# A decoder trunk on one core: the first products put between the transposes of the two halves of the input, and fewer small operations in 1/rms and the final norm

## The chip, the core and the metric

The kernel runs on one core of a Trainium2 chip. The metric is device time in microseconds (us) of one execution, given as the median of three runs. Five engines work beside each other, each through a queue of its own in a fixed order: TensorE (PE; its weight loads are shown as PEld), VectorE (DVE), ScalarE (ACT), GpSimd (POOL), and SyncE (SP), which here only issues transfers. Queues meet at semaphores: an instruction that waits holds up everything behind it on its engine.

## What is computed

The reference is a decoder trunk of two layers on 512 positions with 1024 features. Each layer is a gated linear attention (layer 0) or a stick-breaking attention (layer 1) between two half-step SwiGLU feed-forward blocks; a norm ends it.

```python
def rmsnorm(x, g):
    y = x * lax.rsqrt(jnp.mean(x * x, axis=-1, keepdims=True) + EPS)
    return y * g

def swiglu(h, w_gate, w_up, w_down):
    return (jax.nn.silu(h @ w_gate) * (h @ w_up)) @ w_down

def reference(x, ...):
    for i in range(2):
        x = x + 0.5 * swiglu(rmsnorm(x, ffn1_norm[i]), ffn1_w_gate[i], ffn1_w_up[i], ffn1_w_down[i])
        h = rmsnorm(x, mix_norm[i])
        x = x + (gla_mixer(h, ...) if i == 0 else sb_mixer(h, ...))
        x = x + 0.5 * swiglu(rmsnorm(x, ffn2_norm[i]), ffn2_w_gate[i], ffn2_w_up[i], ffn2_w_down[i])
    return rmsnorm(x, final_norm)
```

The feed-forward width is 2816. Inputs and output are float32.

## The kernel before

**Layout.** The running x is kept transposed in eight tiles `xs[k]` of 128 features by 512 positions. Every product runs on pairs: a value is split into a rounded part (`h`, made by a cast on ACT) and the rest (`l`, value minus `h`, made on DVE), and `mm3` issues three matmuls, `wh*h`, `wl*h` and `wh*l`. One column of 128 outputs over 1024 features is thus 8 x 3 = 24 matmuls of 512 positions, made by `feat`. Its accumulators rotate over eight PSUM banks.

**Feed.** All weight products stand in one list, `feed.q`. Each entry has weights to be split (`split`: `wh` cast on ACT, `wl` subtraction on DVE, four buffers of each) and a generator `body` that issues its matmuls in two halves. Taking an entry with `start` also splits the two that follow and loads further ones.

**The norm.** The products begin before the norm's 1/rms is known: the input is multiplied by the gain alone, the sums of squares run aside, and the factor comes in later. `two_halves(stats_a)` issues the first two columns (48 matmuls) and between their halves `stats_a`, which calls `rstd` for the 1/rms of 512 positions as a 128 x 4 tile (`rv`, square root `ry` on ACT, reciprocal, `rq`, `r4`). `stats_b` makes four diagonal tiles `dg` and multiplies them by ones on PE, which gives `ps_R`, a bank with the factor in every row; `R` is its copy. Then the first two columns, kept back in their banks, are multiplied by `R` (`flush`), and DVE and ACT make the normed tiles `xn`, `nh`, `nl` and their sums and differences `ts`, while PE works on the third to sixth columns. The seventh column is the first that reads `nh` and `nl`. From the third chunk of weights on a scheme with seven products in place of eight is used (`seven`).

**The start.** x arrives as eight blocks (four of positions, two halves of features; SP's queue, with the first weight between the halves). One transpose of the 50 rows of gains gives `gT`. Then, for all eight `k`, four transposes fill a bank, ACT writes `xh` (bank times gain), DVE writes `xl`, and a copy (ACT and DVE by turns) keeps the bank in `xs[k]`. The squares of the blocks run on ACT with their sums in `sums`. The program states the order of few of these; a scheduler places the others, and an `issue_after` in the source puts an instruction behind another one.

**The end.** The last block's down product is made by positions. For each of four position tiles `last` runs twice, for the left (`dh` 0) and the right half: add to x, square with a sum, and after the second half `rstd` of one column, scaling of both halves, and two transfers to the output.

Of the kernel before, what the change touches and what calls it, by code (L numbers as in the profile page):

```python
# [18 lines left out]
P = 128  # L19
T = 512  # L20
# [12 lines left out]
def decoder(ctx: ExitStack, tc: tile.TileContext, a: dict, out: bass.AP):  # L33
# [29 lines left out]
    def mm(ps, l, r, first, last):  # L63
        nc.tensor.matmul(ps, l, r, start=first, stop=last)  # L64
# [27 lines left out]
    class Entry:  # L92
# [8 lines left out]
        def split(self):  # L101
            if self.W is None:
                self.W = []
                for ch, view, n, m in self.units:
# [14 lines left out]
                    st["cut"] = nc.scalar.copy(h, r).ins  # L119
                    with tc.issue_after(st["gains"]):  # L120
                        nc.vector.tensor_tensor(out=l, in0=r, in1=h.bitcast(F32), op=ALU.subtract)  # L121
# [52 lines left out]
    def feat(ch, f, evac, tag=None, defer=None):  # L174


        def body(W):
            (wh, wl), = W
            ps = psum("ps_f", tag)
            for part in (range(0, KD // 2), range(KD // 2, KD)):  # L180
                for k in part:
                    mm3(ps, wh[:, k], wl[:, k], st["h"][k], st["l"][k], k == 0, k == KD - 1)
                if part[-1] == KD - 1:
# [183 lines left out]
    def rstd(sums, n):  # L367
        v = sp.tile([P, n], F32, tag="rv", bufs=2, name="rv")
        nc.vector.tensor_scalar(out=v, in0=sums, scalar1=1.0 / D, scalar2=EPS, op0=ALU.mult, op1=ALU.add)
# [4 lines left out]
        nc.vector.tensor_tensor(out=q, in0=y, in1=y, op=ALU.mult)  # L374
        nc.vector.tensor_tensor(out=q, in0=q, in1=v, op=ALU.mult)
        nc.vector.tensor_scalar(out=q, in0=q, scalar1=-0.5, scalar2=1.5, op0=ALU.mult, op1=ALU.add)
# [17 lines left out]
    def two_halves(between=None):  # L394

        feed.finish()
        g = [feed.start(), feed.start()]
# [24 lines left out]
    class FFN:  # L422
# [10 lines left out]
        def __init__(self, wg, wu, wd, gi, nxt, first=False, last=False):  # L433
# [6 lines left out]
            for group, (c0, c1) in enumerate(self.GROUPS):  # L440
                slots, put = 2 * (c1 - c0), 0
                for i in range(slots):
# [14 lines left out]
                    elif c not in self.SEVEN_UP:  # L457
                        feat(g, f_, self.evac_g, defer=d)
# [194 lines left out]
        def run(self, between=None):  # L653
            with tc.tile_pool(name="hp", bufs=8, reuse_waits="tile") as self.hp, tc.tile_pool(
# [4 lines left out]
                two_halves(stats_a)  # L659
# [509 lines left out]
    def to_tokens(tp):  # L1169
        fin = st["fin"] = tp.tile([P, D], F32, tag="s", bufs=4, name="fin")  # L1170
# [13 lines left out]
    def last(dh, i, ps):  # L1184
# [7 lines left out]
        if dh == 0:  # L1192
            nc.vector.tensor_tensor(out=x, in0=x, in1=fin[:, 0:T], op=ALU.mult)
            return
        s = st["sq"][:, 2 * i : 2 * i + 1]
        nc.vector.tensor_tensor(out=s, in0=s, in1=sq, op=ALU.add)
        r = rstd(s, 1)
        nc.vector.scalar_tensor_tensor(out=x, in0=x, scalar=r, in1=fin[:, T:D], op0=ALU.mult, op1=ALU.mult)
        nc.sync.dma_start(rows[:, T:D], x)
        nc.scalar.activation(xt[i, 0], xt[i, 0], AF.Copy, scale=r)  # L1200
        nc.sync.dma_start(rows[:, 0:T], xt[i, 0])
# [12 lines left out]
    with tc.tile_pool(name="ip", bufs=1) as ip:  # L1214
        gl = ip.tile([P, P], F32, name="gl")
        nc.vector.memset(gl, 0.0)
        row = 0
        for nm in ("ffn1_norm", "mix_norm", "ffn2_norm"):
# [39 lines left out]
        for e in feed.q[:2]:  # L1258
            e.split()
# [53 lines left out]
```

## Time and profile before

| | us |
|---|---|
| runs | 1871.04, 1872.98, 1873.69 |
| median | 1872.98 |
| the profiled execution's own time | 1871.49 |
| its span, first to last instruction | 1869.6 |

In the profile's rows a time is from the span's start. A timeline row has start, duration, engine, source line, operation, output and input tiles with their shape, how many equal ones follow each other (x), and in brackets how long the engine sat idle before it and what ended that. An engine name with q is its queue issuing a transfer. Durations overlap: the next instruction can start before the last one has drained, so prices are taken from start to start. A group's row has a count, busy time and mean.

### The profile page before, as it was taken

To read this page: it belongs to the slowest core of one execution; us is meant where nothing else is said; L and a number is where in the kernel's file an instruction comes from. 1 tells how busy PE (TensorE), PEld (TensorE's weight loads), DVE (VectorE), ACT (ScalarE), POOL (GpSimd) and SP (SyncE) were. 2 spreads that over 40 slices of the span, in tenths; PEclk is the share of its full clock that TensorE was granted. 3 is DMA by queue.
4 is the path that set the end of the run, shared out by engine and by line. 5 is a ranking of instruction groups with operands and counts; after the bars stand their busy time and mean duration, and the time that the engine had idled before them with its cause. 6 is when DMAs were issued, how large, how long until landed. Compare 5 with 4: busy or idle time off the path is not lost.

```text
span 1869.6 us, 28889 instructions
## 1 busy us (share of the span) xinstructions
PE 1849.7 (99%) x11789; PEld 1647.6 (88%) x11789; DVE 1456.8 (78%) x2313; ACT 954.0 (51%) x1506; POOL 7.3 (0%) x17
## 2 busy tenths in 40 slices
PE   8999999999999999999999999999999999999998
PEld 6899999789887899999888999998888788999997
DVE  7978777775766988877888778776878769778785
ACT  6534434444555544444554444445888755444444
POOL 0000000100000000000000000000000000000000
PEclk9999999999999999999999999999999999999999
DMA  5423333212223233342233333233221223333321
GB/s 158 146 91 112 103 113 105 86 50 65 64 72 113 77 104 103 108 129 80 79 113 124 102 102 113 79 93 100 68 68 57 68 91 95 120 102 102 119 85 68
DMA packets 177514, 179.03 MB, mean 96 GB/s; under 512 B 4035, under 2 KB 167925, under 8 KB 177381
## 3 DMA queue, kind: packets, MB, share of 16 engines
q1 hardware_dynamic: 176768, 176.18, 30.1%
q8 instruction: 92, 1.51, 0.3%
q0 software_dynamic: 512, 0.99, 0.2%
q14 instruction: 42, 0.34, 0.1%
q10 hardware_dynamic: 100, 0.03, 0.0%
HBM read 175.11 MB, written 2.10 MB: 95 GB/s over the span
## 4 chain that ended last, share of the span: by engine, by line
PE 96%; DVE 2%; ACT 1%; DMA 1%; issue 0%; DVEq 0%; ACTq 0%; SPq 0%
PE ps_d L64 25%; PE ps_f L64 20%; PE ps_w L510 15%; PE ps_z L510 10%; PE ps_q L510 10%; PE ps_t L64 5%; PE ps_b L64 4%; PE ps_S L64 1%; PE ps_z L1044 1%; PE ps_bt L64 1%; PE ps_oT L1106 1%; PE ps_T L1091 1%; PE ps_o L64 1%; DVE wl L121 0%; DMA raw<-in_ffn_w_up_dram 0%; PE ps_R L64 0%
## 5 line engine op out<-in xcount | busy, mean ns | idle before, releaser
L121 DVE TENSOR_TENSOR wl<-raw,wh 128x1024 fp32r<-128x1024 f32 x244 | 261.3, 1071 | 81.8 <-ACT wh L119 71.6
L119 ACT CAST wh<-raw 128x1024 fp32r<-128x1024 f32 x244 | 226.5, 932 | 137.4 <-PE ps_f L64 44.3
L64 PE MATMUL ps_d<-hh,wl 128*128 128x512 f32 x672 | 262.1, 390 | 0.0
L64 PE MATMUL ps_d<-hh,wh 128*128 128x512 f32 x672 | 262.1, 390 | 0.0
L64 PE MATMUL ps_d<-hl,wh 128*128 128x512 f32 x672 | 261.4, 389 | 0.0
L119 ACT CAST wh<-s 128x1024 fp32r<-128x1024 f32 x136 | 142.8, 1050 | 142.4 <-PE ps_q L510 70.4
L297 DVE SCALAR_TENSOR_TENSOR x<-ps_d,x 128x512 f32<-128x512 f32 x184 | 125.6, 688 | 87.6 <-PE ps_d L64 87.4
L121 DVE TENSOR_TENSOR wl<-s,wh 128x1024 fp32r<-128x1024 f32 x136 | 166.2, 1222 | 25.9 <-ACT wh L119 15.3
L64 PE MATMUL ps_f<-xh,wh 128*128 128x512 f32 x448 | 181.7, 406 | 3.1 <-DVE q L707 1.5
L64 PE MATMUL ps_f<-xl,wh 128*128 128x512 f32 x448 | 175.0, 391 | 0.0
L64 PE MATMUL ps_f<-xh,wl 128*128 128x512 f32 x448 | 174.5, 389 | 0.0
L119 ACT CAST wh<-rawd 128x1024 fp32r<-128x1024 f32 x84 | 88.5, 1054 | 150.7 <-PE ps_d L64 127.6
L510 PE MATMUL ps_z<-th,wh 128*128 128x256 f32 x544 | 150.3, 276 | 0.0
L510 PE MATMUL ps_z<-th,wl 128*128 128x256 f32 x544 | 150.2, 276 | 0.0
L510 PE MATMUL ps_z<-tl,wh 128*128 128x256 f32 x544 | 150.1, 276 | 0.0
L510 PE MATMUL ps_w<-nh,wl 128*128 128x256 f32 x544 | 150.1, 276 | 0.0
L510 PE MATMUL ps_w<-nl,wh 128*128 128x256 f32 x544 | 150.1, 276 | 0.0
L64 PEld LDWEIGHTS ps_d<-hl,wh 128*128 128x128 f32 x672 | 126.2, 188 | 26.7
L64 PEld LDWEIGHTS ps_d<-hh,wh 128*128 128x128 f32 x672 | 126.2, 188 | 24.8
L64 PEld LDWEIGHTS ps_d<-hh,wl 128*128 128x128 f32 x672 | 126.1, 188 | 24.1
L121 DVE TENSOR_TENSOR wl<-rawd,wh 128x1024 fp32r<-128x1024 f32 x84 | 102.9, 1225 | 42.8 <-ACT wh L119 33.6
L510 PE MATMUL ps_w<-nh,wh 128*128 128x256 f32 x488 | 134.7, 276 | 0.0
(249 smaller groups left out, 4711.7 us busy)
## 6 DMA issues: line engine op xcount, KB each, us to landing
raw<-in_ffn_w_gate_dram SPq DMA_DIRECT2D x43, 1024.0 KB, 5.4
raw<-in_ffn_w_up_dram SPq DMA_DIRECT2D x43, 1024.0 KB, 5.3
rawd<-in_ffn_w_down_dram SPq DMA_DIRECT2D x84, 512.0 KB, 3.5
raw<-in_gla_w_in_dram SPq DMA_DIRECT2D x12, 1024.0 KB, 5.3
raw<-in_sb_w_in_dram SPq DMA_DIRECT2D x16, 512.0 KB, 3.8
raw<-in_gla_w_out_dram SPq DMA_DIRECT2D x4, 1024.0 KB, 5.1
raw<-in_sb_w_in_dram SPq DMA_DIRECT2D x4, 1024.0 KB, 5.1
raw<-in_sb_w_out_dram SPq DMA_DIRECT2D x4, 1024.0 KB, 5.0
```

The lines of the kernel that those rows point to most:

```text
L64: nc.tensor.matmul(ps, l, r, start=first, stop=last)
L119: st["cut"] = nc.scalar.copy(h, r).ins
L121: nc.vector.tensor_tensor(out=l, in0=r, in1=h.bitcast(F32), op=ALU.subtract)
L297: nc.vector.scalar_tensor_tensor(out=xs[k], in0=ps, scalar=0.5, in1=xs[k], op0=ALU.mult, op1=ALU.add)
L510: nc.tensor.matmul(o, l_, r_, start=first and j + n == 0, stop=j == 3 and n == 2, skip_group_check=True)
L1044: nc.tensor.matmul(o_, l_, r_, start=first, stop=last, skip_group_check=True)
L1091: nc.tensor.transpose(ps[:, c0 : c0 + P], ys[yb][:, yc + j * P : yc + (j + 1) * P], ident)
L1106: nc.tensor.matmul(po[e * 64 : e * 64 + 64, j * P : T], self.v[j][:, c : c + 64], self.wt[p, e][bk][:, c0 : c0 + n], start=j == 0, stop=j ...
```

## The change

The start is written in an explicit order. The gains come in two tiles, `gls[0]` with the 16 rows that the first block needs and `gls[1]` with the rest. `turn(0)` transposes the left half of the features, then the first gain tile, and writes `xh`, `xl` of `k` 0 to 3. The first weight is split behind the third of these evacuations (`behind` is an `issue_after` on several instructions), the kept copies come behind that split, and the first column's body runs its first part, now three of eight `k` (nine matmuls). Behind the last of them on PE stands `turn(1)` with the right half's sixteen transposes; then the second weight's split, its copies, the splits that `feed.start()` makes, six of the eight squares, the rest of the first column and the second gain transpose. Since the first column is done, `two_halves` takes one column for the first block. In the built kernel ACT's queue runs, from the start: two squares, four `xh`, the first weight's cast, two copies, four `xh`, the second weight's cast, two copies, the third's cast, six squares, the fourth's cast, a table load, the square root and the casts of the fifth, sixth and seventh columns. On DVE the splits of the fifth and sixth columns stand between the reciprocal and the end of 1/rms. On PE `ps_R` stands behind 18 matmuls of the third column. SP's queue keeps its order up to the output. Behind the first 80 us or so the queues are as before until the last norm.

`rstd` keeps the sum of squares undivided (the constants take the factor), can add a second sum in its first operation, and for one column multiplies twice in one operation. `last` writes the left half times the final gain to a tile of its own, `xf`, and sends it from ACT's queue.

```diff
     def mm(ps, l, r, first, last):
-        nc.tensor.matmul(ps, l, r, start=first, stop=last)
+        st["pe"] = nc.tensor.matmul(ps, l, r, start=first, stop=last).ins
...
-                    st["cut"] = nc.scalar.copy(h, r).ins
-                    with tc.issue_after(st["gains"]):
-                        nc.vector.tensor_tensor(out=l, in0=r, in1=h.bitcast(F32), op=ALU.subtract)
+                    st["cut"] = (
+                        nc.scalar.copy(h, r).ins,
+                        nc.vector.tensor_tensor(out=l, in0=r, in1=h.bitcast(F32), op=ALU.subtract).ins,
+                    )
...
-            for part in (range(0, KD // 2), range(KD // 2, KD)):
+            for ks in (range(0, part), range(part, KD)):
...
-    def rstd(sums, n):
+    def rstd(sums, n, more=None):
         v = sp.tile([P, n], F32, tag="rv", bufs=2, name="rv")
-        nc.vector.tensor_scalar(out=v, in0=sums, scalar1=1.0 / D, scalar2=EPS, op0=ALU.mult, op1=ALU.add)
+        nc.vector.tensor_scalar(
+            out=v, in0=sums, scalar1=0.0 if more is None else more, scalar2=D * EPS, op0=ALU.add, op1=ALU.add
+        )
...
-        nc.vector.tensor_tensor(out=q, in0=y, in1=y, op=ALU.mult)
-        nc.vector.tensor_tensor(out=q, in0=q, in1=v, op=ALU.mult)
-        nc.vector.tensor_scalar(out=q, in0=q, scalar1=-0.5, scalar2=1.5, op0=ALU.mult, op1=ALU.add)
+        if n == 1:
+            nc.vector.scalar_tensor_tensor(out=q, in0=y, scalar=v, in1=y, op0=ALU.mult, op1=ALU.mult)
+        else:
+            nc.vector.tensor_tensor(out=q, in0=y, in1=y, op=ALU.mult)
+            nc.vector.tensor_tensor(out=q, in0=q, in1=v, op=ALU.mult)
+        c = float(D) ** 0.5
+        nc.vector.tensor_scalar(out=q, in0=q, scalar1=-0.5 * c, scalar2=1.5 * c, op0=ALU.mult, op1=ALU.add)
...
-                        feat(g, f_, self.evac_g, defer=d)
+                        feat(g, f_, self.evac_g, defer=d, part=3 if len(feed.q) == 0 else KD // 2)
...
-                two_halves(stats_a)
+                two_halves(stats_a, 2 - (feed.pos == 1))
...
         if dh == 0:
-            nc.vector.tensor_tensor(out=x, in0=x, in1=fin[:, 0:T], op=ALU.mult)
+            st["xf"] = st["tp"].tile([P, T], F32, tag="s", bufs=4, name="xf")
+            nc.vector.tensor_tensor(out=st["xf"], in0=x, in1=fin[:, 0:T], op=ALU.mult)
             return
-        s = st["sq"][:, 2 * i : 2 * i + 1]
-        nc.vector.tensor_tensor(out=s, in0=s, in1=sq, op=ALU.add)
-        r = rstd(s, 1)
+        r = rstd(sq, 1, st["sq"][:, 2 * i : 2 * i + 1])
         nc.vector.scalar_tensor_tensor(out=x, in0=x, scalar=r, in1=fin[:, T:D], op0=ALU.mult, op1=ALU.mult)
         nc.sync.dma_start(rows[:, T:D], x)
-        nc.scalar.activation(xt[i, 0], xt[i, 0], AF.Copy, scale=r)
-        nc.sync.dma_start(rows[:, 0:T], xt[i, 0])
+        nc.scalar.activation(st["xf"], st["xf"], AF.Copy, scale=r)
+        nc.scalar.dma_start(rows[:, 0:T], st["xf"])
...
+        def turn(hf):
+            pst = []
+            for k in range(hf * 4, hf * 4 + 4):
+                ps = psum("ps_x")
...
+                pst.append(ps)
+            if hf == 0:
+                ps = psum("ps_g")
+                nc.tensor.transpose(ps[:, 0:P], gls[0], ident)
+                nc.vector.tensor_copy(gT[:, 0:16], ps[:, 0:16])
+            for k, ps in enumerate(pst, hf * 4):
...
+                turned.append(c)
+            return pst
...
+        squares(0, (0, 1))
+        pst = turn(0)
+        with behind(turned[2]):
+            feed.q[0].split()
+        with behind(st["cut"]):
+            keep(pst, 0)
+        body = feed.q[0].body(feed.q[0].W)
+        next(body)
+        with tc.issue_after(st["pe"]):
+            pst = turn(1)
+        with behind(turned[5]):
+            feed.q[1].split()
+        with behind(turned[7]):
+            keep(pst, 1)
+            feed.start()
+        with behind(st["cut"]):
+            squares(0, (2, 3))
+            squares(1, range(NT))
+        for _ in body:
+            pass
+        ps = psum("ps_g")
+        with tc.issue_after(st["pe"]):
+            nc.tensor.transpose(ps[:, 0:P], gls[1], ident)
+        nc.vector.tensor_copy(gT[:, 16:50], ps[:, 16:50])
```

69 lines of the change are left out of this document (37 added, 32 removed).

## The prediction

> **What bounds the kernel now.** I read the page first: TensorE (PE) is busy for nearly the whole span, so only the stretches in which it is idle or slow can pay or cost.
>
> ```profile
> PE 1849.7 (99%) x11789; PEld 1647.6 (88%) x11789; DVE 1456.8 (78%) x2313; ACT 954.0 (51%) x1506; POOL 7.3 (0%) x17
> ```
>
> Of the 1869.6 us span, 20 us are left, and the waits of PE put 6.0 of them before its first instruction. The change touches the first 50 us and the last 8, so I read the timeline of both, PE first.
>
> ```profile
> 6.00 0.45 PE L1234 MATMUL ps_g<-ident,gl 128*128 128x128 f32 x1 [6.00 <-DMA gl<-in_ffn_norm_dram]
> 6.24 3.41 PE L1241 MATMUL ps_x<-ident,x 128*128 128x128 f32 x15
> ```
>
> ```profile
> 12.19 3.00 PE L1241 MATMUL ps_x<-ident,x 128*128 128x128 f32 x13 [0.25 <-DMA x<-in_x_dram]
> 14.87 0.54 PE L64 MATMUL ps_f<-xh,wh 128*128 128x512 f32 x1
> 15.25 0.40 PE L64 MATMUL ps_f<-xh,wl 128*128 128x512 f32 x1
> 15.49 0.40 PE L64 MATMUL ps_f<-xl,wh 128*128 128x512 f32 x1
> ```
>
> ```profile
> 1836.34 3.65 PE L1177 MATMUL ps_T<-ident,x 128*128 128x128 f32 x32
> ```
>
> The reader is to see two speeds. At the end 32 transposes start (3.65-0.27)/31 = 0.109 us apart (0.27: one transpose there); at the start (3.41-0.42)/14 = 0.214 apart. So PE runs at half rate at the start, and it does so until the last transpose; the first products (14.87, 15.25, 15.49) already come at 0.38 and 0.24. Whatever lifts PE to full rate, before has paid it with transposes; the products are spared.
>
> **The change part by part.** The two ends come from different work: the tail is a serial chain, the start is a reordering. The sum is made against the profiled execution's 1871.49 us, which lies 1.49 under the median of 1872.98.
>
> *Tail.* The last tile's chain on VectorE (DVE) loses the addition of the two sums and one of the two multiplications.
>
> ```profile
> 1863.36 0.16 DVE L1196 TENSOR_TENSOR gT<-gT 128x1 f32<-128x1 f32 x1 [0.85 <-ACT ps_bt L1190]
> 1863.55 0.15 DVE L369 TENSOR_SCALAR rv<-gT 128x1 f32<-128x1 f32 x1
> ```
>
> ```profile
> 1864.17 0.16 DVE L374 TENSOR_TENSOR rq<-ry 128x1 f32<-128x1 f32 x1
> 1864.37 0.16 DVE L375 TENSOR_TENSOR rq<-rq,rv 128x1 f32<-128x1 f32 x1
> ```
>
> ```profile
> 1865.69 0.33 SPq L1201 DMA_DIRECT2D out_dram<-x  x1
> 1866.12 0.38 SPq L1199 DMA_DIRECT2D out_dram<-x  x1
> ```
>
> ```profile
> q1 hardware_dynamic: 288, 0.52, 41.0%
> ```
>
> Nothing covers this chain, so each removed step is worth its start-to-start: 0.19 + 0.20 = 0.39 us. The second output transfer goes to ScalarE's (ACT's) queue, so it is issued up to 1866.12-1865.69 = 0.43 earlier. The DMA line covers 1865.5 to 1868.9: 41% of 3.4 us is 1.4 us of all 16 engines for these two transfers, and they ran one behind the other, so a joint issue shares the same engines. I take 0 for it (bounds 0 and -0.43). The issue takes a place in ACT's queue, where only the next tile's first square stands behind it, and nothing behind the last tile's: hidden. Copying into a new tile xf costs nothing: same operation, and its fourth buffer waits for an output sent three tiles earlier. Tail: -0.4 us (bounds -0.2, -0.8). For the four-column 1/rms the number of operations is unchanged, so the other norms give 0.
>
> *Start, step 1: up to the first product.* PE no longer waits for all four gain loads, but the first 16 transposes need the fourth block of x.
>
> ```profile
> 6.34 0.63 ACT L1264 ACTIVATE junk<-x 128x512 f32<-128x512 f32 x1
> 6.49 0.21 DVE L1235 COPY gT<-ps_g 128x50 f32<-128x50 f32 x1 [5.45 <-PE ps_g L1234]
> ```
>
> ```profile
> 9.05 1.05 ACT L119 CAST wh<-raw 128x1024 fp32r<-128x1024 f32 x1 [1.98 <-DMA raw<-in_ffn_w_gate_dram]
> ```
>
> ```profile
> 16.21 1.32 ACT L1246 ACTIVATE xh<-ps_x,gT 128x512 fp32r<-128x512 f32 x2
> 17.36 0.64 ACT L1257 COPY x<-ps_x 128x512 f32<-128x512 f32 x1
> 17.82 1.12 ACT L119 CAST wh<-raw 128x1024 fp32r<-128x1024 f32 x1
> 18.77 0.70 ACT L1264 ACTIVATE junk<-x 128x512 f32<-128x512 f32 x1
> 19.30 0.26 ACT L1264 ACTIVATION_READ_ACCUMULATOR junk<-x 128x1 f32 x1
> 19.39 0.65 ACT L1257 COPY x<-ps_x 128x512 f32<-128x512 f32 x1
> ```
>
> ```profile
> 16.10 2.72 DVE L1247 SCALAR_TENSOR_TENSOR xl<-ps_x,gT,xh 128x512 fp32r<-128x512 f32 x4
> 18.73 1.28 DVE L1255 COPY x<-ps_x 128x512 f32<-128x512 f32 x2
> 19.93 1.22 DVE L121 TENSOR_TENSOR wl<-raw,wh 128x1024 fp32r<-128x1024 f32 x1
> ```
>
> These rows give the start-to-start prices: on ACT an xh (17.36-16.21)/2 = 0.575, a kept copy 0.46, a cast 0.95, a square 0.62; on DVE an xl 0.66, a copy 0.60. The block is read at 6.34 by ACT, so it has landed by then: fourth transpose at 6.3, twelve more at 0.214 end at 8.9, and only then stands the gain transpose, at 9.1. Its copy follows 0.49 later and takes 0.21, so the first xh starts at 9.9 (before: 11.48). But the new order puts all four xh ahead of the first weight's cast: 9.9+4x0.575 = 12.2, although that weight was there at 9.05. The cast ends at 13.25 and frees the first product; wl ends 1.22 later, at 14.5, and the second product waits for it. So the products gain 0.8 us at most (15.25 to 14.5), and behind nine of them stand sixteen transposes that before had behind it by then.
>
> *Step 2: at what rate PE runs there.* After the gain transpose PE is idle from 9.5 to 13.3. I take it to be at half rate at 14.5 again and to need as much unbroken work as before had directly ahead of its first full-rate product: 14.87-12.19 = 2.7 us, so until 17.2. Six products at an estimated 0.44 (0.228 times 0.214/0.109), two at 0.228, sixteen transposes at 0.109: 17.6, then 19.35. Bounds: no slow work after 14.5 (18.1), or slow for 8.9 us as from 6.00 to 14.87 (21.3).
> The Trainium skill ("TensorE: Matmul & The Clock Gate", Part 1) has the rule for this: an idle PE gets half its clock, and gets all of it after a busy window of about 3.4 us that runs free of the kernel. The factor of two agrees with the trace, while the page's clock row (tenths, all 9) does not show the slow spell.
>
> *Step 3: the first two columns.* The second half's xh run at 18.4 and every 0.575, xl behind them at 0.66, and PE uses them in that order: it is the later, 19.35+15x0.228 = 22.8. The second weight is cast at 20.7, its wl is done at 23.0; so no wait, and 0.24 for the second gain transpose plus 24x0.228 put 48 products at 28.5. In before they end where the R product starts, 26.69: 1.8 late.
>
> *Step 4: R.* In the built order of the changed kernel ACT runs after the last xh (to 20.7): cast, two copies, cast, six squares, cast, table load, square root. DVE has two further weight splits (wl, of columns four and five) between the reciprocal and the rest of 1/rms. In before one split stands ahead of the reciprocal and none behind it.
>
> ```profile
> 23.50 1.28 ACT L371 ACT_TABLE_LOAD   x1
> ```
>
> ```profile
> 23.98 1.22 DVE L121 TENSOR_TENSOR wl<-raw,wh 128x1024 fp32r<-128x1024 f32 x1
> 25.11 0.17 DVE L372 RECIPROCAL ry<-ry 128x4 f32<-128x4 f32 x1
> ```
>
> ```profile
> 25.91 0.16 DVE L378 TENSOR_TENSOR r<-ry,rq 128x4 f32<-128x4 f32 x1
> 26.18 0.87 DVE L387 TENSOR_SCALAR dg<-ident,r 128x128 f32<-128x128 f32 x4
> ```
>
> ```profile
> 26.69 1.06 PE L64 MATMUL ps_R<-dg,gT 128*128 128x128 f32 x8
> 27.50 0.47 PE L64 MATMUL ps_f<-xh,wh 128*128 128x512 f32 x1
> 27.78 0.69 DVE L392 COPY R<-ps_R 128x512 f32<-128x512 f32 x1 [0.72 <-PE ps_R L64]
> ```
>
> ACT: 20.7+0.95+0.93+0.95+6x0.62 = 27.25, cast 28.2, table 1.28, root at 29.5, reciprocal at 29.8. The first split waits for its cast, which stands behind the root (29.75+1.05 = 30.8), and takes 1.13; 0.2 for a small operation, the second split 1.13, then 0.4 to r, 0.27 to dg, 0.51 to PE: R at 34.45. PE has done the 18 products that stand ahead of R at 28.5+18x0.228 = 32.6. It waits 1.85 us; queued behind R are the six last products of the third column, and every product after. Next product: 34.45+0.81 = 35.3; in before the same product came at 27.50+18x0.228 = 31.6. Now 3.7 late.
>
> *Step 5: the normed input.* R now comes with 78 products left before the normed tiles are used, in before with 96.
>
> ```profile
> 49.39 0.39 PE L64 MATMUL ps_f<-nh,wh 128*128 128x512 f32 x1
> ```
>
> ```profile
> 48.99 0.76 DVE L608 TENSOR_TENSOR ts<-xn 128x256 f32<-128x256 f32 x2
> 49.70 1.29 DVE L599 TENSOR_TENSOR nl<-xn,nh 128x512 fp32r<-128x512 f32 x2
> ```
>
> DVE works without a break from R's copy (27.78) to the fourth nl (50.39): 22.6 us. PE wants that nl eleven products after 49.39, at 51.9: 1.5 to spare. After: the queue has one split (1.13) and two differences (0.67) less, so 20.8 from 35.55, that is 56.4; PE wants it at 35.3+89x0.228 = 55.6. Another 0.8 us (bounds 0 and 1.5). Behind it DVE is no later than PE by more than that, so nothing further.
>
> Sum: 3.7+0.8-0.4 = +4.1 us: 1875.6 for a profiled execution, 1877.1 as a median. By the bounds of step 2 alone it is +2.7 to +5.6.
>
> **The rivals.**
> *Full rate at once.* The first product already lifts the rate, as 14.87 to 15.25 (0.38, then 0.24) would allow: one product there was enough. Decides if the products from 14.5 on come 0.23 apart. Then transposes end at 18.1, 48 products at 27.2, R (bound by ACT and DVE) at 33.05: +3.1-0.4 = +2.7, 1875.7. That is not slower by a measurement's 0.2% (3.7 us, about what can be told from no change here). For it: the records show full rate from the second product. Against: half rate for 8.9 us just before it.
> *A long slow spell.* PE idles for 3.8 us between 9.5 and 13.3, which never happens in before, and starts afresh: slow to 20.6 or beyond, all nine products and the transposes; 48 products at 30.1 to 30.9, while R moves with them: +5.3 to +5.6, about 1878.4. For it: 8.9 us of half rate from 6.00. Against: that work had waits in it.
> By the skill's window the full clock would come between 17.9 and 21.3 here, an estimate from that page's 3.4 us, which is +4.4 to +5.5 in all.
> *The splits are no obstacle.* If R needed neither split (an idle DVE queue), step 4's wait and step 5's go and +1.5 stays, 1874.5. Against it stands the written order of the queue; nothing for it but error in my durations.
> *Faster by 0.2%.* It would take 3.7 us out of what precedes the second product; the twelve transposes behind the fourth block at full rate would bring the xh forward by 12x0.105 = 1.3, no more. I find no mechanism for it.
>
> **How the numbers follow.** Forecast 0.5, full rate at once 0.22, long slow spell 0.18, no obstacle 0.06, faster 0.04. The forecast lies just above 0.2%, so 0.33 of its 0.5 counts as slower; with 0.18 that makes 0.51; same is 0.17+0.22+0.06 = 0.45; faster 0.04. The range takes in the rivals from 1875.7 to 1878.6 and the spread of the median about them (1.3 us either way): 1874.4 to 1879.9.
>
> **What would show it.** Right: the first product at about 13.3 and the second at 14.5; products 0.4 apart there; a wait of PE for DVE dg of 1 to 2 us at about 33; a short wait for nl at about 56; last DVE chain two operations shorter. Wrong: products at 0.23 from 14.5 on (step 2), no wait at R (step 4), an R product before 32, or an end of 48 products before 27.

## The result, and the profile after

The change makes the kernel slower: 1879.12 us median of seven runs (1877.72 to 1880.09) against 1872.32 us of the kernel before on the same chip, a ratio of 1.0035 with a 95% interval of 1.0023 to 1.0047. That is 6.8 us, where 4.1 were forecast. The profiled execution took 1879.43 us with a span of 1877.7, 8.1 us over the span before. One of the eleven runs of the last experiment below took 1896.99 us at a granted clock of 0.948, and its ratio and interval include that run.

TensorE's line of the page and its timeline at the start, of the changed kernel:

```profile
PE 1853.0 (99%) x11790; PEld 1648.7 (88%) x11790; DVE 1456.3 (78%) x2307; ACT 952.3 (51%) x1506; POOL 7.3 (0%) x17
```

```profile
13.58 0.80 PE L64 MATMUL ps_f<-xh,wh 128*128 128x512 f32 x1 [3.65 <-ACT wh L120]
14.84 0.79 PE L64 MATMUL ps_f<-xh,wl 128*128 128x512 f32 x1 [0.47 <-DVE wl L121]
...
17.56 0.63 PE L64 MATMUL ps_f<-xh,wl 128*128 128x512 f32 x1
17.99 0.47 PE L64 MATMUL ps_f<-xl,wh 128*128 128x512 f32 x1
18.30 1.91 PE L1267 MATMUL ps_x<-ident,x 128*128 128x128 f32 x16
```

PE is no busier in share, but by 3.3 us (1853.0 against 1849.7) with one matmul more: some work ran slowly. The products behind 14.84 come up to 17.99 0.43 us apart (the first of them 0.59), those behind them 0.23, and the sixteen transposes behind them take 1.67 us (18.30 to the next product at 19.97): full rate from about 18.2. The norm's factor, PE and then DVE:

```profile
34.67 1.16 PE L64 MATMUL ps_R<-dg,gT 128*128 128x128 f32 x8 [1.33 <-DVE dg L395]
35.58 0.47 PE L64 MATMUL ps_f<-xh,wh 128*128 128x512 f32 x1
```

```profile
30.38 0.18 DVE L376 RECIPROCAL ry<-ry 128x4 f32<-128x4 f32 x1 [0.29 <-ACT ry L375]
31.31 1.23 DVE L121 TENSOR_TENSOR wl<-raw,wh 128x1024 fp32r<-128x1024 f32 x1 [0.76 <-ACT wh L120]
...
32.53 1.22 DVE L121 TENSOR_TENSOR wl<-raw,wh 128x1024 fp32r<-128x1024 f32 x1
...
34.33 0.87 DVE L395 TENSOR_SCALAR dg<-ident,r 128x128 f32<-128x128 f32 x4
```

The two splits stand where the forecast put them, between the reciprocal and the rest of 1/rms. The product behind R starts at 35.58; the same one started at 31.71 before, so PE is 3.9 us late. At the normed input two short waits follow:

```profile
54.51 0.50 PE L64 MATMUL ps_f<-nh,wl 128*128 128x512 f32 x1 [0.51 <-DVE wl L121]
...
57.37 0.51 PE L64 MATMUL ps_f<-nl,wh 128*128 128x512 f32 x1 [0.21 <-DVE nl L607]
```

Set against the same products of before, PE is 4.0 us late at 50 us and 5.4 at 60. It stays there, within 0.2 us, for 540 us. Then comes a place that the forecast did not look at: the first products of layer 0's second feed-forward block. PE's timeline there, of before and then of after, and windows of after (length, busy time of PE, PEld, DVE, ACT and POOL with counts, the granted clock, the share of the DMA engines, GB/s):

```profile
599.39 0.50 PE L64 MATMUL ps_f<-xh,wh 128*128 128x512 f32 x1 [1.20 <-DVE x L232]
...
605.19 0.97 PE L64 MATMUL ps_st<-gT,ss 128*128 128x1 f32 x8
```

```profile
610.74 1.05 PE L64 MATMUL ps_st<-gT,ss 128*128 128x1 f32 x8 [1.31 <-DVE ss L342]
...
612.72 0.63 PE L64 MATMUL ps_f<-xh,wh 128*128 128x512 f32 x1
613.14 0.63 PE L64 MATMUL ps_f<-xh,wl 128*128 128x512 f32 x1
```

```profile
608.67:612.08 3.41, 2.10 (x14) 1.59 (x13) 1.48 (x4) 1.97 (x3) 0.00 (x0) 1.00 1.07 348
612.08:615.49 3.41, 3.41 (x10) 2.63 (x9) 2.85 (x10) 1.19 (x2) 0.00 (x0) 0.50 0.15 48
```

The reader is to see a wait that changed its place. Before, PE waits 1.20 us in front of the second column. In the changed kernel the scheduler has ordered the first products of these two columns otherwise (twelve and twelve, where before had eight, twelve and four), the wait in front of the second column is gone, and 1.31 us of it come back in front of the eight small products that sum the squares. That alone would be even. But behind them the granted clock falls to 0.50 for 3.41 us, and eight products come 0.43 us apart. PE is 4.1 us late ahead of this wait, 5.6 at the first product behind the sums and 7.2 behind those eight: 1.8 us over the lateness at 60 us, of which the slow spell is 1.6. So the description's sentence that the queues behind the first 80 us are as before until the last norm was wrong at this place. At 717 and 1086 us 0.3 and 0.7 us more are lost at short waits of the attention products, and 0.2 are won back behind them; the trace of the tail alone, which has the start of before, loses 0.3 and 0.5 at these places too, so they are not put down to the start. The end:

```profile
1871.33 0.21 DVE L371 TENSOR_SCALAR rv<-gT 128x1 f32<-128x1 f32 x1 [0.79 <-ACT ps_bt L1200]
...
1872.02 0.22 DVE L379 SCALAR_TENSOR_TENSOR rq<-ry,rv 128x1 f32<-128x1 f32 x1
...
1873.40 0.37 ACTq L1210 DMA_DIRECT2D out_dram<-xf  x1
1873.43 0.33 SPq L1208 DMA_DIRECT2D out_dram<-x  x1
```

From PE's last product (1869.43, before 1861.39) to the first of the last two issues it is 3.97 us, before 4.30; to the end of the span it is 8.23, before 8.16. The chain is shorter and the end is not: from the first issue to the last landing it is 2.83 us, before 2.72, and from there to the end of the span 1.42, before 1.14.

### The profile page after: what moved, and what is told of

Read it like the earlier page. It is cut to its first block, busy times and chain, and to the rows that moved or that the text cites. A ratio compares the mean times of both kernels' runs of the same rounds, so it can differ in the third digit from the quotient of the medians.

```text
span 1877.7 us, 28872 instructions
## 1 busy us (share of the span) xinstructions
PE 1853.0 (99%) x11790; PEld 1648.7 (88%) x11790; DVE 1456.3 (78%) x2307; ACT 952.3 (51%) x1506; POOL 7.3 (0%) x17
## 3 DMA queue, kind: packets, MB, share of 16 engines
q8 instruction: 92, 1.51, 0.3%
## 4 chain that ended last, share of the span: by engine, by line
PE 93%; DVE 3%; DMA 1%; ACT 1%; SPq 1%; issue 0%; ACTq 0%; DVEq 0%
PE ps_d L64 24%; PE ps_f L64 18%; PE ps_w L518 14%; PE ps_z L518 10%; PE ps_q L518 10%; PE ps_t L64 5%; PE ps_b L64 4%; PE ps_S L64 1%; PE ps_z L1053 1%; PE ps_bt L64 1%; PE ps_oT L1115 1%; PE ps_T L1100 1%; PE ps_o L64 1%; DVE wl L121 1%; SPq L89 1%; DMA rawd<-in_ffn_w_down_dram 0%
## 5 line engine op out<-in xcount | busy, mean ns | idle before, releaser
L64 PE MATMUL ps_d<-hh,wl 128*128 128x512 f32 x672 | 262.2, 390 | 0.0
L64 PE MATMUL ps_d<-hh,wh 128*128 128x512 f32 x672 | 262.2, 390 | 0.0
L64 PE MATMUL ps_d<-hl,wh 128*128 128x512 f32 x672 | 261.5, 389 | 0.0
L64 PE MATMUL ps_f<-xh,wh 128*128 128x512 f32 x448 | 183.2, 409 | 5.2 <-ACT wh L120 3.7
L64 PE MATMUL ps_f<-xh,wl 128*128 128x512 f32 x448 | 176.0, 393 | 0.5 <-DVE wl L121 0.5
L64 PE MATMUL ps_f<-xl,wh 128*128 128x512 f32 x448 | 176.4, 394 | 0.0
L64 PEld LDWEIGHTS ps_d<-hl,wh 128*128 128x128 f32 x672 | 126.2, 188 | 26.7
L64 PEld LDWEIGHTS ps_d<-hh,wh 128*128 128x128 f32 x672 | 126.2, 188 | 24.8
L64 PEld LDWEIGHTS ps_d<-hh,wl 128*128 128x128 f32 x672 | 126.2, 188 | 24.1
```

What stands on the lines that cost most here:

```text
L64: st["pe"] = nc.tensor.matmul(ps, l, r, start=first, stop=last).ins
```

## The experiments

Medians are against the kernel before on the same chip (1871.99, 1872.33 and 1872.24 us in the three sets). "Late" means PE's start of a product against the same product of another kernel's trace.

### The tail alone, and the start alone

The kernel before with the new `rstd` and `last`:

> The kernel before with the change's rstd and final norm alone (two small operations fewer in the last chain, the left half sent from ACT's queue from a tile of its own). By the prediction's tail step: the last chain 0.35 us shorter and the span 0.3 to 0.4 us shorter than before, which is within the noise of the median. Rival, from the profile of the changed kernel, where the two last transfers landed 2.6 and 2.8 us after their issue and in before 2.0 and 2.3: two transfers issued together land later, and nothing of the 0.35 is left, 0 to -0.1. Both: -0.0 to -0.4 us.

1873.25 us, ratio 1.0007 (0.9998 to 1.0016): 1.3 us over before by the medians, where 0 to 0.4 under it were expected. The chain to the first issue is 3.98 us here too; the transfers landed 3.7 and 3.5 us after their issue, later than in either kernel; the last experiment shows what lay in the way.

The changed kernel with the old `rstd` and `last`:

> The changed kernel with the rstd and the final norm of before: the start's new order alone. If the start carries the whole loss: +6.8 to +7.2 us to before (6.8 of the changed kernel plus up to 0.4 of the tail). If the tail's transfers or the new rstd carry part of it: under +6.

1878.69 us, ratio 1.0036 (1.0023 to 1.0049), 6.7 us over before. The start carries the loss; the tail is worth nothing, or a fraction of a microsecond to the bad. The drop of the clock at 612 us is in this trace as well.

### PE kept busy behind the gain transpose

```diff
                 nc.vector.tensor_copy(gT[:, 0:16], ps[:, 0:16])
+                for _ in range(15):
+                    nc.tensor.transpose(ps[:, P : 2 * P], ident, ident)
```

> The changed kernel with 15 transposes of the identity on PE behind the first gain transpose, into an unused part of its bank: PE is no longer idle from 9.9 to 13.6 us. If idleness is what brings the half rate back, the nine products behind 14.8 run 0.23 apart instead of 0.43, the second transposes start 1.6 us earlier and the whole run is 1.3 to 1.6 us shorter than the changed kernel (about +5.3 to before). Rival: transposes don't count as work for the clock, and the products stay at 0.43 apart: no gain, +6.8.

1875.45 us, ratio 1.0019 (1.0010 to 1.0028), 3.7 under the changed kernel. PE at the start, and ACT and PE in front of the sums at 600 us:

```profile
10.18 2.16 PE L1277 MATMUL ps_g<-ident 128*128 128x128 f32 x15 [0.27 <-DVE gT L1275]
13.57 0.50 PE L65 MATMUL ps_f<-xh,wh 128*128 128x512 f32 x1 [1.23 <-ACT wh L121]
14.83 0.50 PE L65 MATMUL ps_f<-xh,wl 128*128 128x512 f32 x1 [0.76 <-DVE wl L122]
...
16.80 1.91 PE L1268 MATMUL ps_x<-ident,x 128*128 128x128 f32 x16
```

```profile
595.23 2.00 ACT L121 CAST wh<-raw 128x1024 fp32r<-128x1024 f32 x2 [4.60 <-DMA raw<-in_ffn_w_up_dram]
```

```profile
608.10 1.05 PE L65 MATMUL ps_st<-gT,ss 128*128 128x1 f32 x8 [0.20 <-DVE ss L343]
```

The first and second product start where they did (13.57, 14.83), and all products from there on run at full rate: the transposes start 1.50 us earlier, and 1.5 us is what PE is ahead until 590 us. Step 2's half rate is real, its cause is what PE did before, and transposes on the identity count as work for it. The rest of the 3.7 us was not expected: the queues at 600 us are in the same order as in the changed kernel, but the weight that the two casts at 595.23 wait for took 5.3 us from issue to landing, in the changed kernel and before 6.4. So the chain of additions behind it was 2.6 us ahead instead of 1.5, the sums' wait 0.20 us instead of 1.31, and no clock fell. The cast's row in the changed kernel names another releaser, a product (`597.87 ... [5.71 <-PE ps_b L64]`), but that came at almost the same time; the load had been issued at 591.36 and landed at 597.79.

The DMA queues show what made the load slower. While it is in flight in the changed kernel (591.36 to 597.80), and then in this one (589.83 to 595.16):

```profile
q8 instruction: 1, 0.02, 0.9%
raw<-in_ffn_w_up_dram SPq DMA_DIRECT2D x1, 1024.0 KB, 6.4
```

```profile
raw<-in_ffn_w_up_dram SPq DMA_DIRECT2D x1, 1024.0 KB, 5.3
```

In the changed kernel one packet of queue q8, of 16 KB and 0.9 us, runs among the load's packets, and the load's last sixteen come one after another about 1 us late. In this kernel that packet ran 2.1 us before the load was issued. It is so in all thirteen traces: with the packet in flight the load took 6.4 to 6.8 us (nine traces), without it 5.3 to 5.4 (this one, the warmed kernel and both repaired ones). q8 has 92 such packets for PE's 23,580 products and weight loads, about 256 to a packet, so it most likely brings PE's program; and versions with 15, 22 and 39 more transposes on PE ahead of this place have the packet 4.5, 5.2 and 9.5 us earlier against the load. By that the filling did two things, and the second, with the spell that it avoided, was luck. No experiment moved the packet alone.

### The first weight's cast ahead of the four evacuations

```diff
+                c = nc.vector.tensor_copy(gT[:, 0:16], ps[:, 0:16]).ins
+                with tc.issue_after(c):
+                    feed.q[0].split()
...
-        with behind(turned[2]):
-            feed.q[0].split()
```

> The changed kernel with the first weight's cast on ACT at 9.05 us, ahead of the four xh in place of behind them, and its split on DVE behind the gain copy. If the order of evacuations is what delays the products: first product at 10.9 (13.6 in the changed kernel), second at 11.4 (14.8), nine done at 14 to 16 (18.3), and with ACT's later work and R also 2.5 to 4 us earlier: +3 to +4.5 to before. Rival: R is bound by something that does not move (loads of the third and fourth column), and the gain is under 1 us.

1876.24 us, ratio 1.0022 (1.0012 to 1.0031), 2.9 under the changed kernel.

```profile
10.89 0.80 PE L64 MATMUL ps_f<-xh,wh 128*128 128x512 f32 x1 [0.99 <-ACT xh L1281]
...
14.81 0.63 PE L64 MATMUL ps_f<-xl,wh 128*128 128x512 f32 x1
15.24 2.27 PE L1267 MATMUL ps_x<-ident,x 128*128 128x128 f32 x16
```

The first product comes 2.7 us earlier and all nine run slowly: the half rate now lasts 5.1 us, from the first product (10.89) to some way into the transposes (15.98). PE waits 1.00 us for dg at 32 us, because that chain moves by 2.7 us as well. PE gains 2.7 us by 60 us, and the medians 2.9, within the expectation; R was not bound by something that does not move. At 608 us it waits 1.36 us for the sums, and the clock falls as in the changed kernel.

### The two splits held until 1/rms is done

DVE's subtractions of the fifth and sixth column are put behind the last `dg`:

```diff
-                        nc.vector.tensor_tensor(out=l, in0=r, in1=h.bitcast(F32), op=ALU.subtract).ins,
+                        self.sub(l, r, h),
...
+        def sub(self, l, r, h):
+            with tc.issue_after(st["late"]) if st.get("late") else ExitStack():
+                return nc.vector.tensor_tensor(out=l, in0=r, in1=h.bitcast(F32), op=ALU.subtract).ins
```

> The changed kernel with one thing altered: VectorE's two weight splits that stood between the reciprocal and the rest of 1/rms (columns five and six) are held until the four diagonal blocks (dg) are done. Theory of step 4: these two splits (start to start 2.75 us from the reciprocal at 30.4 to r at 34.1, less about 0.8 for the small operations) are what PE waits for at R. Then dg is ready 2.2 us earlier, the wait of 1.33 us at R is gone and the product behind R starts 1.3 to 1.4 us earlier. The two splits now stand behind dg and push the normed input back by about 1.1 us relative to R, so that its wait (0.5 and more at 54 us) grows; net -0.2 to -1.4 us against the changed kernel, about 1878.2. Rival: R waits for the square root on ScalarE (28.8 to 30.3) and the splits only fill the time; then the wait stays above 1 us and the time is the changed kernel's.

1875.68 us, ratio 1.0020 (1.0010 to 1.0029), 3.4 under the changed kernel by the medians; its profiled span is 1875.9, 1.8 under.

```profile
30.61 0.18 DVE L380 RECIPROCAL ry<-ry 128x4 f32<-128x4 f32 x1 [0.29 <-ACT ry L379]
...
31.42 0.16 DVE L390 TENSOR_TENSOR r<-ry,rq 128x4 f32<-128x4 f32 x1
```

```profile
32.03 1.16 PE L64 MATMUL ps_R<-dg,gT 128*128 128x128 f32 x8 [0.38 <-DVE dg L399]
```

From the reciprocal to r it is 0.81 us instead of 3.68, and R starts at 32.03 instead of 34.67. The scheduler used this: 57 products stand ahead of R instead of 66, so a wait of 0.38 us is left. Having reached this stretch 0.35 us later, PE is 0.6 us ahead of the changed kernel behind R, and 1.4 ahead behind the normed input, where the wait of 0.51 us is gone: the better end of the expectation, though by another way, since the normed input was expected to wait longer.

The rest of the difference of the medians is not explained by this trace. It is of the longest of the ten runs (1877.73 us; the others took 1875.04 to 1876.29) and has the slow spell at 610 us (its sums waited 1.26 us) and a longer half rate at the start:

```profile
9.22:12.63 3.41, 0.21 (x2) 0.00 (x0) 2.41 (x5) 2.95 (x5) 0.00 (x0) 1.00 1.10 346
12.63:19.46 6.83, 5.91 (x17) 4.56 (x18) 2.86 (x4) 1.82 (x4) 0.00 (x0) 0.50 1.13 319
```

Here the first transposes had brought the full clock at 9.22; it was lost again in the gap before the first product (13.08), and all nine products and half of the transposes behind them ran at half rate, to 19.46. Whether the other nine were spared one or both of these is not shown.

### Two trials of the clock at 612 us

Eleven identity transposes ahead of the sums of squares:

```diff
             ps = psum("ps_st", tag)
+            for _ in range(11 if second_call else 0):
+                nc.tensor.transpose(ps[:, P : 2 * P], ident, ident)
```

> The changed kernel with eleven extra identity transposes on PE ahead of the sums of squares at about 609 us (the eight 128x1 products that waited 1.3 us for VectorE there). They fill the wait and change no result. Theory: the lower clock granted from 612 to 616 us (eight products 0.43 us apart instead of 0.23) follows from PE standing idle for 1.3 us and then running small work; with PE kept busy the clock stays whole there, the products stay 0.23 apart, and the time falls by 1.6 to 1.9 us against the changed kernel, to about 1877.3. Rival: the small 128x1 products or the other engines bring the clock down whatever PE does before; then products are 0.43 apart at the same place and the time is the same or up to 0.3 us longer.

1880.47 us, ratio 1.0045 (1.0030 to 1.0060). This trial missed its aim:

```profile
607.91 1.36 PE L365 MATMUL ps_st<-ident 128*128 128x128 f32 x11
...
611.45 1.05 PE L64 MATMUL ps_st<-gT,ss 128*128 128x1 f32 x8 [1.47 <-DVE ss L342]
```

The scheduler put the transposes three products ahead of the wait, so they filled nothing; the wait of 1.47 us and the slow spell (612.8 to 616.2) stayed. It tells neither theory from the other.

The same sums with 128 columns instead of one:

```diff
-                mm(ps[:, i : i + 1], st["ss"][:, i * P : (i + 1) * P], ones[:, 0:1], True, True)
-            sums = ps[:, 0:NT]
+                mm(ps[:, i * P : (i + 1) * P], st["ss"][:, i * P : (i + 1) * P], ones, True, True)
+            sums = ps.rearrange("p (n m) -> p n m", m=P)[:, :, 0]
```

> The changed kernel with one size altered: the products that sum the squares (ps_st) have 128 columns instead of 1, all alike, and the first of each is read. They run 0.11 us apart in either size, so they cost no time themselves; the order of the queues is the same. Theory one: the lower clock after 611 us follows from a wait of 1.3 us together with eight products that give TensorE next to nothing to do (128x1), about 2.2 us of little work in all; waits of 1.2 and 1.5 us in front of full products, at 599 and 371 us in the kernel before, were followed by none. Then with 128 columns the products after the wait stay 0.23 us apart and the time falls by 1.6 to 2 us against the changed kernel, to 1877.3. Theory two: the wait of 1.3 us by itself is enough there; the eight slow products stay, and so does the time, 1879.

1877.93 us, ratio 1.0032 (1.0020 to 1.0044), 1.2 under the changed kernel.

```profile
611.08 1.16 PE L64 MATMUL ps_st<-gT,ss 128*128 128x128 f32 x8 [1.68 <-DVE ss L342]
...
612.54 0.40 PE L64 MATMUL ps_f<-xl,wh 128*128 128x512 f32 x1
612.77 0.40 PE L64 MATMUL ps_f<-xh,wh 128*128 128x512 f32 x1
```

```profile
612.46:615.87 3.41, 3.41 (x19) 2.82 (x18) 2.85 (x10) 1.40 (x3) 0.00 (x0) 1.00 0.14 46
```

The wait is even longer, 1.68 us, and no clock falls: products 0.23 apart, clock 1.00. From 0.3 us behind the changed kernel at the sums it goes to 1.1 ahead at 614, a gain of 1.5. So it is not the wait alone. (The queues stand in the same order, and the load at 591 us took 6.8 us, so the place is as it was in the changed kernel.)

A rival is that the clock looks at fixed stretches of time, and that the wait fell into them otherwise. The traces' record of the clock settles it: between its first and its last change every stretch of half or full clock is a multiple of 3.41 us (3.41, 6.83, 10.24, 593.92), whatever PE does, so it does go by steps of a fixed length. But in the changed kernel the wait and the small products lie within the step ahead of the fall (608.67 to 612.08), and so, to within 0.3 us, they do in the other four kernels with a spell. Here the wait and the wide products lie within one step as well (609.05 to 612.46), and the clock stays. The rival is out.

In the five profiled kernels whose eight 128x1 products followed a wait of 1.26 us or more, a slow spell followed (the changed one, the start alone, the early cast, the held splits, the extra transposes); behind waits of 0 to 0.3 us none did, and none behind waits of 1.20 and 1.51 us in front of full products at 599 and 371 us in before. (Those two fall on two steps each; in the changed kernel the second, at 376 us, lies within one step, and no spell follows there either.) "TensorE: Matmul & The Clock Gate", Part 1 of the Trainium skill, has the clock fall after an idle window of about 3.4 us. Here the idling was 1.3 us, and with the small products 2.2 (1.31 and 0.91) of a step of 3.41. By the runs 128x1 products count as little work, and 2.2 us of it was enough; where the limit lies was not measured.

### The kernel before with PE warmed from 1.4 us on

```diff
         ps = psum("ps_g")
+        for _ in range(22):
+            nc.tensor.transpose(ps[:, P : 2 * P], ident, ident)
         nc.tensor.transpose(ps[:, 0:P], gl, ident)
```

> The kernel before with 22 extra identity transposes on PE ahead of its first gain transpose (PE has nothing to do until 6.0 us and the identity is there at 1.3). Theory: PE's half rate at the start is a matter of how long it has been busy; warmed from 1.4 us on, its 33 transposes from 6.0 run 0.11 us apart, the first product comes about 1.3 us earlier (13.5 instead of 14.87). What it is worth in the end is bounded by VectorE: dg was done at 26.5 and R used at 26.7, so PE would wait for dg by about 1 us and only 0.2 us would be left: 1872.1, and a wait for DVE dg of about 1 us in the waits. Rival: the half rate belongs to the first microseconds of a run and not to idleness; then transposes at 6.2 are 0.214 apart as before and the time is the same or longer.

1875.90 us, ratio 1.0022 (1.0012 to 1.0032): slower than before by 3.6.

```profile
1.36 4.96 PE L1236 MATMUL ps_g<-ident 128*128 128x128 f32 x22 [1.36 <-POOL ident masks.py:199]
...
6.39 2.27 PE L1244 MATMUL ps_x<-ident,x 128*128 128x128 f32 x16
...
18.52 0.80 PE L65 MATMUL ps_f<-xh,wh 128*128 128x512 f32 x1 [4.65 <-ACT x L1260]
```

```profile
14.02 1.04 ACT L120 CAST wh<-raw 128x1024 fp32r<-128x1024 f32 x1 [2.28 <-DMA raw<-in_ffn_w_up_dram]
```

The warming worked: the first half's sixteen transposes take 2.27 us, where fifteen took 3.41 in before, with the step to full rate at about 7.1. But the added work made the scheduler place the second weight's cast and a square ahead of all xh on ACT; the cast waited for its load until 14.02, the evacuations behind it too, PE sat idle 4.65 us and ran its next thirteen products slowly. The rival (half rate belongs to the first microseconds) is out; what warming is worth in that order was not measured.

### All repairs together

The changed start with the early cast, the held splits, identity transposes from 1.4 us on (11, 2, 6 and 2 ahead of the four blocks of x, 18 behind the gain transpose), eleven ahead of the sums at 609 us, and the old tail:

> The changed order at the start with every repair at once: the first weight cast ahead of the evacuations, the two splits held behind dg, identity transposes on PE from 1.4 us on (11, 2, 6, 2 ahead of the four blocks of x, 18 behind the gain transpose) and eleven at 609 us; 1/rms and the last norm as in the kernel before. If the four causes found so far are all there is (half rate at the start about 1.5, the late cast about 2.5, the splits about 0.7, the clock at 612 about 1.9), the time is 1879.1 - 6.6 = 1872.5, level with the kernel before, with the first product at 10.5 to 11 us and products 0.23 apart from the start. If the new order has a cost of its own besides (banks, queues), it stays above 1874. If the clock could be had earlier than any kernel had it, down to 1870.

1871.97 us, ratio 1.0000 (0.9990 to 1.0010), 0.5 under the 1872.5 of the sum of the four causes. The same without the eleven and with the wide sums:

> The kernel with every repair at the start again (first weight cast first, two splits held behind dg, identity transposes from 1.4 us on), without the eleven transposes before the sums of squares, which came 1.2 us too early there and only lengthened PE's queue, and with the sums of squares 128 columns wide. If the eleven transposes cost what they last and the sums' wait stays without a slow spell, it is 0.9 to 1.2 us under the version with them (1871.97): about 1871.0, 0.07% under the kernel before. If PE's wait for the sums only grows by what the transposes took, the time is the same, 1872.

1870.08 us (1869.05 to 1870.78), ratio 0.9988 (0.9980 to 0.9997): 2.2 us under the kernel before and 9 under the changed one. It beats both.

```profile
1.36 2.61 PE L1268 MATMUL ps_x<-ident 128*128 128x128 f32 x11 [1.36 <-POOL ident masks.py:199]
...
6.77 1.64 PE L1269 MATMUL ps_x<-ident,x 128*128 128x128 f32 x13
...
10.78 0.50 PE L66 MATMUL ps_f<-xh,wh 128*128 128x512 f32 x1
```

The thirteen transposes behind the fourth block start in 1.48 us (6.77 to 8.25) instead of 2.83, the first product comes at 10.78 and products run at full rate. Behind the normed input PE is 0.7 us ahead of before, ahead of 599 us 0.3, and behind the sums 1.25, since the wait of 1.20 us is gone there and the sums wait 0.3. But in both repaired kernels the load ahead of that place met no packet of q8 and took 5.3 to 5.4 us. So of the lead in this trace 1.0 us may be owed to that and not to the repairs; the runs do not separate the two. Against their own runs of before it gained 1.8 us on the version with the eleven transposes (-2.2 against -0.4), where 0.9 to 1.2 were expected; where the rest is from stays open.

### The shorter chain with both output transfers on one queue

```diff
-        nc.scalar.dma_start(rows[:, 0:T], st["xf"])
+        nc.sync.dma_start(rows[:, 0:T], st["xf"])
```

> The kernel before with the shorter chain of the last norm alone (two small VectorE operations fewer, a tile of its own for the first half), and both output transfers on the one queue of SyncE as before. If the loss of the tail came from two queues at once (landing 2.6 to 3.7 us after issue instead of 2.0 to 2.3), the transfers land 2.0 to 2.3 us after issue and the 0.39 us of the small operations shows: end 0.4 us nearer to PE's last product (7.8 instead of 8.16) and -0.4 us in the time. If landings differ from run to run for reasons of their own, the end lies 7.7 to 9 us behind the last product and the time shows nothing.

1872.60 us, ratio 1.0016 with an interval of 0.9992 to 1.0039: inconclusive by time (the medians differ by 0.4 us). The groups of output transfers (instruction count, KB of each, median us from issue to landing) of before, of the changed kernel and of this one:

```profile
out_dram<-x SPq DMA_DIRECT2D x8, 256.0 KB, 2.2
```

```profile
out_dram<-xf ACTq DMA_DIRECT2D x4, 256.0 KB, 2.8
out_dram<-x SPq DMA_DIRECT2D x4, 256.0 KB, 2.6
```

```profile
out_dram<-xf SPq DMA_DIRECT2D x4, 256.0 KB, 2.1
out_dram<-x SPq DMA_DIRECT2D x4, 256.0 KB, 2.3
```

On two queues at once a transfer takes 0.3 to 0.7 us longer to land than on one queue, one behind the other. The last pair is the only one that counts: 2.83 and 2.63 us in the changed kernel, 2.02 and 2.29 in before. In three of the profiles (this one, the tail alone, the eleven transposes) the last pair landed 0.9 to 1.2 us later still, on one queue as on two. In these three, and in none of the other ten, a packet of another queue for instructions (q14, 8 KB) ran among the pair's packets, 1.9 us after the first issue. The other ten agree closely: with two queues (five traces) the span ends 8.22 to 8.23 us behind PE's last product, with one queue and the old chain (five) 8.15 to 8.17. So the tail as built costs 0.07 us. The shorter chain on one queue was seen only with the packet in the way (8.82), so what it is worth by itself stays open.

## Why the prediction was right, and where it was not

**The direction** held, and the time lies in the range, but the size owes something to luck. By its own steps the start lost 5.4 us where 4.5 were forecast. The 8.1 us between the two profiled spans are these 5.4, 1.8 at 600 us, 0.8 at the attention products and 0.1 at the tail; a third of it comes from places that are not in the sum. The range reached as far up as 1879.9 for the sake of the long slow spell at the start, and that is not what filled it.

**Step 1** held within 0.35 us: first xh at 10.17 (forecast 9.9), first product at 13.58 (13.25), second at 14.84 (14.5). The early cast shows the reason, too: without the four evacuations ahead of it the first product comes at 10.89.

**Step 2** named the right mechanism; its rule for the length was wrong. Forecast were 2.7 us of half rate from the second product on, to 17.2, because that much unbroken work stood ahead of the first full-rate product of before; measured are 3.3, to about 18.2, so eight slow products instead of six. The transposes end at 19.97 (19.35). "Full rate at once" is refuted by the slow rows from 14.84 on, and the spell to 20.6 by the full-rate rows from 18.3 on; that the time came out near that rival's 1878.4 has another cause, at 600 us. But neither number is a property of the kernel: in five traces with this start (the changed kernel, the start alone, the held splits, the eleven transposes, the wide sums) the full clock comes at 18.2, 19.5, 19.5, 18.9 and 18.5. And the start of before, read as paying for the clock with its transposes, does not always do so: in the traces of the tail alone and of the one queue, which have it too, the clock was full for 3.41 us from 8.6 and 9.1, then half again until 15.4 and 15.9, into the first products. The windows of the Trainium skill's page ("TensorE: Matmul & The Clock Gate", Part 1: a busy window of about 3.4 us that runs free of the kernel) reach from 17.9 to 21.3 and hold all five. Over the runs PE needed 3.6 us (identity transposes from 1.36, full at 4.95), 4.6 (13.58 to 18.2), 5.1, 5.7 (18.52 to 24.2) and 6.4 us of work (held splits), so no fixed length would have served; the free-running window fits this spread, and the steps of 3.41 us in the record of the clock agree with it.

**Step 3:** 48 products done at 28.5 by the forecast; the next one started at 29.09. The 0.6 us are what the transposes ended late in step 2.

**Step 4** held best: a wait of 1.85 us for dg forecast, 1.33 measured since PE came later; R at 34.67 against 34.45; next product 3.9 us late against 3.7. Holding the two splits left 0.38 us of the stall, so "the splits are no obstacle" is refuted by a run.

**Step 5** is mis-sized: 0.8 us forecast (bounds 0 and 1.5), 1.4 measured, in two waits where one was seen. The first of them (54.51) is for a weight's split, not for the normed input: the same full DVE queue had that to deliver too.

**What was missed** is the sentence "Behind it DVE is no later than PE by more than that, so nothing further". At 600 us the wait of 1.20 us of before was in reach of any shift of the order, and behind the sums of squares it cost twice: as a wait and as a slow spell. The wide sums took the spell away at equal order and brought back 1.5 of its 1.6 us. That there was a wait to turn into a spell hung on the load at 591 us, which met a packet of q8; in the filled kernel, where that packet ran earlier, the sums waited 0.20 us.

**The tail** was forecast at -0.4 us. The chain shrank by 0.33 (the merged operations take 0.21 and 0.22 us against 0.15 and 0.16, so less than the 0.39), but "a joint issue shares the same engines, I take 0" put at nothing what the runs show as a loss. The last landing comes 0.1 us later behind the first issue (2.83 us against 2.72), and 0.3 us more go between it and the end of the span, which lies 8.23 us behind PE's last product instead of 8.16; what takes the 0.3 was not found. For the landings the Trainium skill has a reason ready ("DMA: Bandwidth & Descriptors", "Rules for kernel authors": issuing from several engines only saves issue time, as all run on the same sixteen engines and interleave); the landings above agree with it.

## What to carry to other kernels

Price a reordering by what PE does in the gap it opens: a few microseconds without work cost again behind the gap, at half rate, and cheap transposes on a constant tile can fill it. Then look past the place of the change for every wait that sits in front of small work: here 1.3 us of waiting in front of 128x1 products cost 1.6 us more behind them. And where a scheduler orders the queues, compare the whole built order, since even work that was added as filling moved a cast ahead of what everybody waited for. Last, when a version gains more than its edit explains, look at the DMA queues for instructions: the versions with added products had their packets at other times, and a packet in the way of a load or of the last output was worth about a microsecond.

## What the runs showed of the hardware

- Transposes on the identity raise PE's clock like products do: from 0.213 us apart to 0.109 after 3.6 us (the repaired version) and 5.8 us (before, warmed). The Trainium skill ("TensorE: Matmul & The Clock Gate", Part 4) says that the full clock does not engage for them; here it did.
- The clock changes by steps of 3.41 us: every stretch of half or full clock between two changes is a multiple of it, and where the steps begin differs from execution to execution.
- The clock fell in the middle of a kernel after about 2.2 us of idling and 128x1 products within one such step, for 3.41 us, and did not fall when the same products had 128 columns.
- One and the same weight load took 6.4 to 6.8 us with a 16 KB packet of the queue q8 for instructions in flight, and 5.3 to 5.4 without. In the filled kernel the quick load left the sums a wait of 0.20 us and no spell came; in before the slow load brought none either, since its wait stood in front of full products.
